# Reordering the linear pieces between a mixer's attentions, pacing the modulation by product work, and moving the first weight casts of a section

## The chip, the cores and the metric

The kernel runs on one core of a Trainium2 chip. The metric is the device time of one execution in microseconds (us). A run "before" means the kernel without the change; its median of three runs is 1349.51 us.

## The reference, cut to what matters

A trunk of two layers on one sequence of 256 tokens, 1024 wide. Each layer is a feed-forward half step, a token mixer, and a second feed-forward half step:

```python
def swiglu(h, w_gate, w_up, w_down):
    return (jax.nn.silu(h @ w_gate) * (h @ w_up)) @ w_down          # 1024 -> 2816 -> 1024
...
    proj = hn @ w_in                                                # 1024 -> 3488 + 3 * 1024 gates
    y_a = from_heads(moba_attention(...))                           # 256 tokens: causal softmax attention
    y_b = from_heads(stick_breaking_attention(qb_, kb_, vb_))
    qc = to_heads(rms_norm(c_q, q_norm) @ w_uq, MLA_HEADS)          # "up" products of the third attention
    kv = to_heads(rms_norm(c_kv, kv_norm) @ w_ukv, MLA_HEADS)
    y_c = from_heads(causal_softmax_attention(...))
    g = jax.nn.sigmoid(gates.reshape(bsz, s_len, N_BRANCH, D_MODEL) + b_gate)
    ys = jnp.stack([y_a, y_b, y_c], axis=2)
    merged = jnp.einsum('bsnk,nkd,bsnd->bsd', ys, w_branch, g)      # three branch products, each times its gate
    return merged @ w_out
...
    for l in range(DEPTH):
        mod = (c_act @ ada_w[l] + ada_b[l])                         # shift, scale, gate of each of the 3 sub-layers
        h = modulate(x, norm_pre[l, 0], mod[:, 0, 0], mod[:, 0, 1])
        x = residual_add(x, swiglu(h, ...), norm_post[l, 0], mod[:, 0, 2], 0.5)
        ...
```

Each of the 2 x 9 modulation vectors is a 1024 x 1024 matrix times one vector, some 75 MB of weights in all.

## The kernel before, in words

Everything lies transposed, 128 channels by 256 tokens to a tile. **Weights** come in pieces of 128 x 1024 f32 (512 KB) through one helper, `wsplit` (L144): SP issues the DMA into `raw` (L153, 5 buffers), ACT casts it to `whi` (L162, 6 buffers), DVE takes the difference `wlo` (L163, 6 buffers). **Products** are three matmuls each (L168 whi by hi, L169 whi by lo, L170 wlo by hi), called "lin"; a piece of 128 output channels from 1024 inputs is 24 matmuls of 256 columns. PSUM has 3 banks for lin, 4 for attention ("att"), one for sums ("sum").

**Modulation.** Behind the first two vectors, which the opening computes from its own loads (`oada`), 128 tiles `ada` of 512 KB are loaded by DMAs that POOL issues (L130, 2 buffers); each is reduced by one DVE instruction, the "dot" (L118). `ada_until(l, s, part)` emits loads and dots up to a share `part` of the 24 tiles that belong to a sub-layer. In the feed-forward it is called once per piece. In the mixer it is called by `progress()`, every second piece, with the count of pieces setting the share. A dot is held behind an "anchor", the last marked DVE instruction. The dots stand in DVE's queue in the place that this gives them, so a dot whose load has not landed holds up all of DVE.

**Mixer.** Three attentions run one after the other through `attend(fn, q, k, v, box, fill)`: stick-breaking (1), softmax (2, the MoBA branch), and softmax of the latent branch (3). Each has four pairs of heads in a pipeline of six steps; in each step a share of the list `fill` of independent linear pieces is emitted between the attention's own instructions. The kinds of pieces: `gate_pieces` (8 of 24 matmuls, evacuated by ACT, L482; behind the eighth one sigmoid over 128 x 2048, L484, between two table loads, L484 and L86), `branch_pieces` (8 of 12 matmuls, evacuated by DVE as a product with the gate, L498, and for branch 0 an addition, L733), `up_pieces` (12 short ones, evacuated by ACT: rot L689, yT L684, km L704, vm L711), `chunk_pieces` and `token_pieces`. After the third attention come branch 2 and the product with `w_out`, four groups of two output tiles, evacuated by `out_tile` (squares L213 and L308, yT L309, both ACT, and DVE for the last).

**Section changes.** `enter` normalises and modulates for the next section. Its list `hold` keeps instructions behind which the casts of the weights (both L162 and L163) must stand.

Instructions have the order that a scheduler gives them by the order in which the program emits them, with `issue_after` and `high_priority` as exceptions; on each engine they then run strictly in that order.

Of the kernel before, what the change touches and what calls it, by code (L numbers as in the profile page):

```python
# [12 lines left out]
F32R = mybir.dt.float32r  # L13
BF = mybir.dt.bfloat16
AF = mybir.ActivationFunctionType
# [4 lines left out]
S = 256  # L20
# [8 lines left out]
def trunk(ctx, tc, x, c, vecs, ada_w, w_gate, w_up, w_down, w_in, w_uq, w_ukv, w_branch, w_out, rope, out):  # L29
# [94 lines left out]
    def ada_until(l, s, part):  # L124

        n = min(24 * (3 * l + s) + int(24 * part), len(ada_todo))
        while ada_pos[0] < n:
            al, i, k = ada_todo[ada_pos[0]]
            raw = adap.tile([128, D], F32, name="ada")
            nc.gpsimd.dma_start(raw, ada_w[al, i * D + k * 128:i * D + k * 128 + 128, :])  # L130
            with tc.issue_after(anchor[-1].ins):
                ada_dot(raw, al, i, k)
            if k == KC - 1:
                nc.vector.tensor_add(modc[:, al, i, :], modc[:, al, i, :], adab[:, al, i * KC:i * KC + KC])
            ada_pos[0] += 1

    hold = []

    def block(src, at, kc, ncols):
# [163 lines left out]
    def out_tile(n, p, g):  # L303
        if n < KC - 1:
            if n < KC - 2:
                sum_sq(sqp, p, n == 0)
            else:
                nc.scalar.activation(sqm, p, AF.Square)  # L308
            nc.scalar.activation(yT[:, n, :], p, AF.Copy, scale=g[:, n:n + 1])  # L309
        else:  # L310
            nc.scalar.activation(sql, p, AF.Square)
            nc.vector.tensor_scalar(yT[:, n, :], p, g[:, n:n + 1], None, op0=OP.mult)
# [4 lines left out]
    def ffn(l, f, s, opening=None, ahead=None):  # L317
        with ExitStack() as es:
# [66 lines left out]
            for g in range(D // 256):  # L385
# [7 lines left out]
                for j in range(2):  # L393
                    out_tile(2 * g + j, pp[j], gc)
                ada_until(l, s, 1)


    def mixer(l, s):
        with ExitStack() as es:
# [184 lines left out]

            def attend(fn, q, k, v, box, fill):

                hi = mp.tile([128, 4, S], F32R, name="ybhi", bufs=2)
                lo = mp.tile([128, 4, S], F32R, name="yblo", bufs=2)
                box["act"] = lambda i, k: (hi, lo)[i][:, k, :]
                gens, wts = {}, {}  # L590
                NS = 6
                done, spent, total = 0, 0.0, sum(w for w, _ in fill)
                for t in range(NS):
                    n = t - 2
                    if n >= 0:
                        y = ps(S, kind="sum")
                        weighted(y, wts.pop(n), v, 2 * n)
                        nc.scalar.copy(hi[:, n, :], y)
                        nc.vector.tensor_sub(lo[:, n, :], y, hi[:, n, :].bitcast(F32))
# [5 lines left out]
                    while done < len(fill) and (spent < total * (t + 1) / NS or t == NS - 1):  # L605
                        spent += fill[done][0]
                        fill[done][1]()
                        done += 1
                        progress()

            steps = [0]

            def progress():
                steps[0] += 1
                if steps[0] % 2 == 0:
                    ada_until(l, s, min(1.0, max(0, steps[0] - 14) / 54))


            wb = [win(1536 + 256 * i, 256) for i in range(3)]
# [112 lines left out]
            def add_a(m):  # L732
                nc.vector.tensor_add(gb["g"][:, m, :], gb["g"][:, m, :], ga["g"][:, m, :])  # L733


            attend(softmax_pair, of64(qka, 0), of64(qka, 4), va, ya,
                   up_pieces() + gate_pieces(1, "ga", gb) + branch_pieces(1, yb, gb))


            attend(softmax_pair, lambda h: qm[:96, h, :], lambda h: km[:96, h, :], vm, yc,  # L740
                   gate_pieces(0, "gb", ga) + branch_pieces(0, ya, ga, add_a) + gate_pieces(2, "gb", gc))
            table_after(SQRT, last_exp[0], gc["sig"])

            def add_c(m):
# [4 lines left out]

            for _, piece in branch_pieces(2, yc, gc, add_c):  # L750
                piece()
            ada_until(l, s, 1)
            gcol = post_col(l, s, 1.0)
            for g in range(4):
                if g == 2:
# [7 lines left out]
                        lin(pp[j], w, k0, cols[j], hact, k0, nk, k0 == 0, k0 + nk == KC)  # L763
                for j in range(2):
                    out_tile(2 * g + j, pp[j], gcol)
                ada_until(l, s, 1)
        return ahead


# [189 lines left out]
```

## Time and profile before

| | |
|---|---|
| runs before, us | 1349.01, 1349.51, 1356.35 (median 1349.51) |
| the profiled execution, us | 1353.12 |
| its span, us | 1351.4 |
| mean granted TensorE clock | 0.984 of full speed |
| busy: PE / DVE / ACT / POOL | 96% / 73% / 56% / 5% |
| DMA | 295.75 MB, mean 219 GB/s |

All positions below are us from the start of that span. The profile names engines PE (TensorE), DVE (VectorE), ACT (ScalarE), POOL (GpSimd) and SP (SyncE). "out<-in" are the program's tiles. Behind an instruction the brackets give the idle time of its engine just ahead of it and the instruction or DMA that ended it. A busy PE need not be at full pace: the granted clock and the number of matmuls in a window tell that.

### The profile page before, as it was taken

To read this page: it belongs to the slowest core of one execution; us is meant where nothing else is said; L and a number is where in the kernel's file an instruction comes from. 1 tells how busy PE (TensorE), PEld (TensorE's weight loads), DVE (VectorE), ACT (ScalarE), POOL (GpSimd) and SP (SyncE) were. 2 spreads that over 40 slices of the span, in tenths; PEclk is the share of its full clock that TensorE was granted. 3 is DMA by queue.
4 is the path that set the end of the run, shared out by engine and by line. 5 is a ranking of instruction groups with operands and counts; after the bars stand their busy time and mean duration, and the time that the engine had idled before them with its cause. 6 is when DMAs were issued, how large, how long until landed. Compare 5 with 4: busy or idle time off the path is not lost.

```text
span 1351.4 us, 26656 instructions
## 1 busy us (share of the span) xinstructions
PE 1303.2 (96%) x10752; PEld 1269.9 (94%) x10752; DVE 986.4 (73%) x1706; ACT 755.7 (56%) x1287; POOL 69.5 (5%) x139
## 2 busy tenths in 40 slices
PE   6999989999899999999999999999998999999997
PEld 5999989998799999999999999999987999999997
DVE  7988766757768879876589775676686777885552
ACT  4554554766656656454565554467575756644551
POOL 0011000000101000110001110000010010000000
PEclk9999998999999999999999999999998999999998
DMA  9988872534866647887829887535366585285560
GB/s 362 343 296 305 281 263 91 188 104 163 287 200 221 229 140 248 306 289 248 274 61 319 292 286 251 195 121 169 118 227 206 194 291 202 80 316 187 173 198 32
DMA packets 82925, 295.75 MB, mean 219 GB/s; under 512 B 9201, under 2 KB 9585, under 8 KB 82802
## 3 DMA queue, kind: packets, MB, share of 16 engines
q1 hardware_dynamic: 64370, 226.94, 49.0%
q0 software_dynamic: 18432, 67.12, 15.1%
q8 instruction: 84, 1.38, 0.4%
q14 instruction: 39, 0.32, 0.1%
HBM read 292.97 MB, written 1.05 MB: 218 GB/s over the span
## 4 chain that ended last, share of the span: by engine, by line
issue 49%; PE 42%; DVE 3%; POOL 3%; DMA 2%; ACT 1%; SPq 0%; POOLq 0%; DVEq 0%; ACTq 0%
PE lin L168 11%; PE lin L170 11%; PE lin L169 11%; POOL ada L130 3%; PE att L823 1%; PE lin L273 1%; DMA ada<-in_ada_w_dram 1%; PE att L273 1%; PE lin L823 1%; PE sum L509 1%; DMA oada<-in_ada_w_dram 1%; PE att L519 1%; PE att L544 0%; DVE ada L118 0%; ACT whi L162 0%
## 5 line engine op out<-in xcount | busy, mean ns | idle before, releaser
L163 DVE TENSOR_TENSOR wlo<-raw,whi 128x1024 fp32r<-128x1024 f32 (+3 forms) x382 | 452.5, 1197 | 148.1 <-ACT whi L162 143.7
L162 ACT CAST whi<-raw 128x1024 fp32r<-128x1024 f32 (+3 forms) x382 | 391.3, 1032 | 227.0 <-PE lin L169 158.3
L170 PE MATMUL lin<-h,wlo 128*128 128x256 f32 x1808 | 510.4, 283 | 0.8 <-DVE wlo L163 0.8
L168 PE MATMUL lin<-h,whi 128*128 128x256 f32 x1808 | 510.9, 284 | 0.1
L169 PE MATMUL lin<-h,whi 128*128 128x256 f32 x1808 | 507.6, 282 | 0.2
L170 PEld LDWEIGHTS lin<-h,wlo 128*128 128x128 f32 x1808 | 341.4, 189 | 1.4 <-DVE wlo L163 1.4
L169 PEld LDWEIGHTS lin<-h,whi 128*128 128x128 f32 x1808 | 341.8, 189 | 1.0 <-DVE h L238 1.0
L168 PEld LDWEIGHTS lin<-h,whi 128*128 128x128 f32 x1808 | 340.4, 189 | 1.8 <-ACT h L237 1.0
L118 DVE SCALAR_TENSOR_TENSOR ada<-ada,cb 128x1024 f32<-128x1024 f32 x128 | 154.6, 1220 | 37.3 <-DMA ada<-in_ada_w_dram 37.0
L168 PE MATMUL lin<-mid,whi 128*128 128x256 f32 x592 | 163.6, 276 | 3.4 <-ACT yT L309 3.4
L170 PE MATMUL lin<-mid,wlo 128*128 128x256 f32 x592 | 163.5, 276 | 0.0
L169 PE MATMUL lin<-mid,whi 128*128 128x256 f32 x592 | 163.5, 276 | 0.0
L130 POOL DMA_DIRECT2D ada<-in_ada_w_dram x128 | 67.8, 530 | 1135.8 <-DVE ada L118 1103.3
L168 PEld LDWEIGHTS lin<-mid,whi 128*128 128x128 f32 x592 | 111.1, 188 | 3.6 <-ACT yT L309 3.6
L170 PEld LDWEIGHTS lin<-mid,wlo 128*128 128x128 f32 x592 | 111.2, 188 | 0.0
L169 PEld LDWEIGHTS lin<-mid,whi 128*128 128x128 f32 x592 | 111.2, 188 | 0.0
L346 ACT CAST mid<-m 128x256 fp32r<-128x256 f32 x88 | 34.7, 405 | 77.9 <-DVE m L342 77.5
L168 PE MATMUL lin<-ybhi,whi 128*128 128x256 f32 x192 | 56.2, 293 | 13.0 <-DVE ga L498 10.9
L169 PE MATMUL lin<-yblo,whi 128*128 128x256 f32 x192 | 54.6, 285 | 0.0
L170 PE MATMUL lin<-ybhi,wlo 128*128 128x256 f32 x192 | 54.5, 284 | 0.0
L168 PEld LDWEIGHTS lin<-ybhi,whi 128*128 128x128 f32 x192 | 37.5, 195 | 15.0 <-DVE ga L498 11.3
L273 PE MATMUL lin<-h,whi 128*128 128x258 f32 x240 | 46.7, 302 | 4.9 <-DVE h L262 4.9
(259 smaller groups left out, 1952.8 us busy)
## 6 DMA issues: line engine op xcount, KB each, us to landing
ada<-in_ada_w_dram POOLq DMA_DIRECT2D x128, 512.0 KB, 5.1
raw<-in_mix_w_in_dram SPq DMA_DIRECT2D x100, 512.0 KB, 5.1
raw<-in_ffn_w_gate_dram SPq DMA_DIRECT2D x88, 512.0 KB, 5.6
raw<-in_ffn_w_up_dram SPq DMA_DIRECT2D x88, 512.0 KB, 5.6
raw<-in_ffn_w_down_dram SPq DMA_DIRECT2D x80, 512.0 KB, 5.1
raw<-in_mix_w_branch_dram SPq DMA_DIRECT2D x24, 512.0 KB, 4.9
oada<-in_ada_w_dram SPq DMA_DIRECT2D x16, 512.0 KB, 7.4
raw<-in_mix_w_out_dram SPq DMA_DIRECT2D x16, 512.0 KB, 5.1
```

The source lines that it names most:

```text
L118: return nc.vector.scalar_tensor_tensor(raw, raw, 1.0, cb, op0=OP.mult, op1=OP.mult, accum_out=modc[:, l, i, k:k + 1])
L130: nc.gpsimd.dma_start(raw, ada_w[al, i * D + k * 128:i * D + k * 128 + 128, :])
L162: nc.scalar.copy(hi, raw)
L163: nc.vector.tensor_sub(lo, raw, hi.bitcast(F32))
L168: nc.tensor.matmul(o, whi, ahi, start=start, stop=False)
L169: nc.tensor.matmul(o, whi, alo, start=False, stop=False)
L170: nc.tensor.matmul(o, wlo, ahi, start=False, stop=stop)
L273: done.append(nc.tensor.matmul(p, w(i, k, cols), (hi, lo)[j], start=(k == 0 and i == j == 0), stop=(k == KC - 1 and j == 1)))
L346: nc.scalar.copy(mid[0][n], m)
L509: nc.tensor.matmul(y[64 * j:64 * j + 64, 128 * t:S], v[:, t, (h + j) * 64:(h + j) * 64 + 64], wT[j][:, 0:S] if t == 0 else wT[j][:, S:S + ...
L519: nc.tensor.matmul(scs[j][:, 128:384], q[j][:, 128:256], k[j][:, 0:256], start=False, stop=False, skip_group_check=True)
L823: nc.tensor.matmul(banks[j][:, a * 256:(a + 1) * 256], parts[k][a][i == 1][:, j * 128:(j + 1) * 128], hact(i == 2, k), start=(k == 0 and a ...
```

## The change

It has five parts. (1) The fill lists: attention 2 has gate 1, the up pieces and gate 0 instead of the up pieces, gate 1 and branch 1; attention 3 has branch 1, branch 0 and gate 2 instead of gate 0, branch 0 and gate 2. (2) `attend` allocates its result tiles `ybhi`/`yblo` in step 2 and not at its start, since three such pairs would be alive with two buffers. (3) `progress` gets a piece's weight (2.6 for 24 matmuls) and asks for `0.85 * (work - 16) / 105` of the 24 dots after every piece; the last dots are asked for behind the first and second group of `w_out` instead of ahead of `w_out`. (4) The first ada tile is written by a small POOL copy that reads the last modulation column of the opening, so its load, and all behind it on POOL, waits for the opening's last dot. (5) `out_tile` notes the evacuation of tile 5 as `late`, and at the end of a feed-forward and of a mixer `hold` is set to it, so the casts of the next section's first weights stand behind that evacuation.

```diff
@@ ada_until @@
             raw = adap.tile([128, D], F32, name="ada")
+            if ada_pos[0] == 0:
+                nc.gpsimd.tensor_copy(raw[:, 0:1], modc[:, 0, 0, KC - 1:KC])
             nc.gpsimd.dma_start(raw, ada_w[al, i * D + k * 128:i * D + k * 128 + 128, :])
...
+    late = []
     hold = []
@@ out_tile @@
-            nc.scalar.activation(yT[:, n, :], p, AF.Copy, scale=g[:, n:n + 1])
+            done = nc.scalar.activation(yT[:, n, :], p, AF.Copy, scale=g[:, n:n + 1])
+            if n == KC - 3:
+                late[:] = [done]
@@ ffn, at its end @@
                 ada_until(l, s, 1)
+            hold[:] = late
@@ attend @@
-                hi = mp.tile([128, 4, S], F32R, name="ybhi", bufs=2)
-                lo = mp.tile([128, 4, S], F32R, name="yblo", bufs=2)
-                box["act"] = lambda i, k: (hi, lo)[i][:, k, :]
...
                     n = t - 2
+                    if n == 0:
+                        hi = mp.tile([128, 4, S], F32R, name="ybhi", bufs=2)
+                        lo = mp.tile([128, 4, S], F32R, name="yblo", bufs=2)
+                        box["act"] = lambda i, k: (hi, lo)[i][:, k, :]
...
                         fill[done][1]()
+                        progress(fill[done][0])
                         done += 1
-                        progress()
-
-            steps = [0]
-
-            def progress():
-                steps[0] += 1
-                if steps[0] % 2 == 0:
-                    ada_until(l, s, min(1.0, max(0, steps[0] - 14) / 54))
+
+            work = [0.0]
+
+            def progress(w):
+
+                work[0] += w
+                ada_until(l, s, 0.85 * min(1.0, max(0.0, work[0] - 16) / 105))
@@ mixer @@
             attend(softmax_pair, of64(qka, 0), of64(qka, 4), va, ya,
-                   up_pieces() + gate_pieces(1, "ga", gb) + branch_pieces(1, yb, gb))
+                   gate_pieces(1, "ga", gb) + up_pieces() + gate_pieces(0, "gb", ga))
...
             attend(softmax_pair, lambda h: qm[:96, h, :], lambda h: km[:96, h, :], vm, yc,
-                   gate_pieces(0, "gb", ga) + branch_pieces(0, ya, ga, add_a) + gate_pieces(2, "gb", gc))
+                   branch_pieces(1, yb, gb) + branch_pieces(0, ya, ga, add_a) + gate_pieces(2, "gb", gc))
...
             for _, piece in branch_pieces(2, yc, gc, add_c):
                 piece()
-            ada_until(l, s, 1)
             gcol = post_col(l, s, 1.0)
...
-                ada_until(l, s, 1)
+                ada_until(l, s, 1 if g else 0.93)
+            hold[:] = late
```

**DVE, layer 0, up to the first branch-1 evacuations.** `gcol` is the mixer's post-norm column, `yblo` the low part of an attention result, `ga<-lin,ga` a branch-1 evacuation. Before:

```order
L297 SCALAR_TENSOR_TENSOR gcol<-modc,vecs 128x8
L118 SCALAR_TENSOR_TENSOR ada,modc<-ada,cb 128x1024
L163 TENSOR_TENSOR wlo<-raw,whi 128x1024
L118 SCALAR_TENSOR_TENSOR ada,modc<-ada,cb 128x1024
L599 TENSOR_TENSOR yblo<-sum,ybhi 128x256
L163 TENSOR_TENSOR wlo<-raw,whi 128x1024
L118 SCALAR_TENSOR_TENSOR ada,modc<-ada,cb 128x1024
L498 TENSOR_TENSOR ga<-lin,ga 128x256 x4
```

The same place now; line numbers are a few higher (L166 is `wlo`, L504 the branch evacuation, L537, L541 and L543 the softmax):

```order
L300 SCALAR_TENSOR_TENSOR gcol<-modc,vecs 128x8
L606 TENSOR_TENSOR yblo<-sum,ybhi 128x256
L166 TENSOR_TENSOR wlo<-raw,whi 128x1024 x4
L537 TENSOR_REDUCE nm<-att 128x1 x2
L504 TENSOR_TENSOR ga<-lin,ga 128x256 x3
L537 TENSOR_REDUCE nm<-att 128x1 x2
L504 TENSOR_TENSOR ga<-lin,ga 128x256
L166 TENSOR_TENSOR wlo<-raw,whi 128x1024
L541 RECIPROCAL r<-sm 128x2 x2
L504 TENSOR_TENSOR ga<-lin,ga 128x256
```

The dot that stood right ahead of the evacuations is elsewhere; softmax instructions of attention 3 now stand among them.

**ACT, layer 0, gate 1's last evacuation and the first two pairs of up pieces** (`rot`, `yT`), now:

```order
L488 ACTIVATE ga<-lin,vecs 128x256
L165 CAST whi<-raw 128x1024
L490 ACT_TABLE_LOAD
L490 ACTIVATE ga<-ga 128x2048
L86 ACT_TABLE_LOAD
L696 ACTIVATE rot<-lin 128x256 x2
L691 ACTIVATE yT<-lin 64x256 x2
L605 CAST ybhi<-sum 128x256
L691 ACTIVATE yT<-lin 64x256 x2
L552 COPY wT<-att 128x384
L691 ACTIVATE yT<-lin 64x256 x4
L552 COPY wT<-att 128x384
```

Before, what followed gate 1's sigmoid on ACT was the attention's own work and casts, with branch 1 on DVE:

```order
L482 ACTIVATE ga<-lin,vecs 128x256
L598 CAST ybhi<-sum 128x256
L484 ACT_TABLE_LOAD
L484 ACTIVATE ga<-ga 128x2048
L86 ACT_TABLE_LOAD
L546 COPY wT<-att 128x384 x2
L162 CAST whi<-raw 128x1024 x2
L598 CAST ybhi<-sum 128x256
```

The block of table load, sigmoid and table load has moved from ahead of casts and copies to ahead of the up evacuations, which free PE's lin banks.

**ACT, the end of the first feed-forward** (with the numbers of the tiles, since rows read alike; `lin_2238` and `lin_2239` hold output tiles 4 and 5). Before:

```order
L162 CAST wd16_0_2536<-raw_2542 128x512
L162 CAST whi_2597<-raw_2595 128x1024
L162 CAST whi_2603<-raw_2601 128x1024
L213 ACTIVATE sq_2408<-lin_2238 128x256
L309 ACTIVATE yT_139<-lin_2238,gcol_1865 128x256
L162 CAST whi_2609<-raw_2607 128x1024
```

Now:

```order
L165 CAST wd16_0_2537<-raw_2543 128x512
L216 ACTIVATE sq_2409<-lin_2239 128x256
L312 ACTIVATE yT_139<-lin_2239,gcol_1866 128x256
L216 ACTIVATE sq_2413<-lin_2240 128x256
L312 ACTIVATE yT_139<-lin_2240,gcol_1866 128x256
L165 CAST whi_2598<-raw_2596 128x1024
```

The casts of the mixer's first weights have moved from ahead of the evacuation of tile 4 to behind that of tile 5.

## Rows read from the trace of the kernel before

**Rows 1.** The page, part 1: busy time, share of the span and instructions of each engine.

```profile
PE 1303.2 (96%) x10752; PEld 1269.9 (94%) x10752; DVE 986.4 (73%) x1706; ACT 755.7 (56%) x1287; POOL 69.5 (5%) x139
```

**Rows 2.** PE's waits over the span: line waited at, instruction waited for, us in total, times, longest.

```profile
PE lin L168 <- DVE ga L498: 10.9, 2, 6.3
...
PE lin L168 <- ACT yT L309: 3.4, 1, 3.4
...
PE lin L168 <- DVE gb L498: 2.0, 2, 1.0
PE lin L168 <- ACT yT L684: 1.5, 4, 0.6
```

**Rows 3.** Windows at the end of attention 2 of layer 0 (363 to 378 us) and layer 1 (1023 to 1035 us). Columns: from and to, length, busy us (and instructions) of PE, weight loads, DVE, ACT, POOL; granted clock; DMA share; GB/s.

```profile
363.30:368.10 4.80, 0.15 (x3) 0.03 (x1) 2.19 (x5) 1.27 (x3) 0.12 (x1) 0.80 0.98 373
368.10:373.10 5.00, 5.00 (x23) 4.07 (x24) 2.64 (x5) 2.46 (x3) 0.40 (x1) 0.51 0.62 202
373.10:378.10 5.00, 5.00 (x46) 5.00 (x45) 2.24 (x5) 0.46 (x1) 0.00 (x0) 1.00 0.67 212
1023.40:1029.80 6.40, 0.18 (x2) 0.00 (x0) 2.58 (x5) 1.33 (x3) 0.40 (x2) 0.89 0.88 319
1029.80:1035.20 5.40, 5.36 (x24) 4.43 (x25) 3.04 (x5) 2.46 (x3) 0.47 (x1) 0.50 0.31 102
```

**Rows 4.** The timeline of DVE in the same two places: start, us, instruction, and in brackets the idle time ahead of it and what ended it.

```profile
366.45 1.23 DVE L118 SCALAR_TENSOR_TENSOR ada<-ada,cb 128x1024 f32<-128x1024 f32 x1 [2.60 <-DMA ada<-in_ada_w_dram]
...
367.60 1.08 DVE L498 TENSOR_TENSOR ga<-lin,ga 128x256 f32<-128x256 f32 x3
...
1028.22 1.23 DVE L118 SCALAR_TENSOR_TENSOR ada<-ada,cb 128x1024 f32<-128x1024 f32 x1 [3.82 <-DMA ada<-in_ada_w_dram]
```

**Rows 5.** The timeline of POOL: the first two ada loads, and the load that the dot at 366.45 us reads.

```profile
2.06 0.67 POOL L130 DMA_DIRECT2D ada<-in_ada_w_dram  x1
...
2.98 0.55 POOL L130 DMA_DIRECT2D ada<-in_ada_w_dram  x1
...
360.39 0.53 POOL L130 DMA_DIRECT2D ada<-in_ada_w_dram  x1 [3.04 <-DVE ada L118]
```

**Rows 6.** The timelines of ACT and PE at the end of the first feed-forward.

```profile
193.47 1.05 ACT L162 CAST whi<-raw 128x1024 fp32r<-128x1024 f32 x1 [2.26 <-DMA raw<-in_mix_w_in_dram]
195.59 1.04 ACT L162 CAST whi<-raw 128x1024 fp32r<-128x1024 f32 x1 [1.07 <-DMA raw<-in_mix_w_in_dram]
196.54 0.38 ACT L213 ACTIVATE sq<-lin 128x256 f32<-128x256 f32 x1
...
197.33 0.39 PE L168 MATMUL lin<-mid,whi 128*128 128x256 f32 x1 [3.43 <-ACT yT L309]
```

**Rows 7.** One window of the opening (columns as in rows 3).

```profile
5.00:10.00 5.00, 1.16 (x2) 0.00 (x0) 2.26 (x5) 1.02 (x3) 0.00 (x0) 1.00 1.00 380
```

**Rows 8.** The timeline of DVE at its first dot of the opening.

```profile
12.72 1.22 DVE L118 SCALAR_TENSOR_TENSOR oada<-oada,cb 128x1024 f32<-128x1024 f32 x1 [1.06 <-DMA oada<-in_ada_w_dram]
```

**Rows 9.** Two windows in the mixer of layer 0 (columns as in rows 3): the up pieces, and eight branch-0 pieces in attention 3.

```profile
317.40:328.80 11.40, 10.60 (x77) 8.45 (x75) 10.47 (x23) 10.01 (x31) 0.53 (x1) 1.00 0.30 93
411.00:423.00 12.00, 11.97 (x103) 11.09 (x103) 11.85 (x30) 9.25 (x18) 0.53 (x1) 1.00 0.79 260
```

**Rows 10.** ACT's instructions by line and shape, 300 to 460 us: count, busy us, mean ns of one, idle ahead.

```profile
L162 ACT CAST whi<-raw 128x1024 fp32r<-128x1024 f32 x42 | 43.8, 1054 | 24.0 <-PE lin L169 21.8 <-PE lin L170 2.1
...
L482 ACT ACTIVATE ga<-lin,vecs 128x256 f32<-128x256 f32 x8 | 3.9, 487 | 2.0 <-PE lin L170 2.0
...
L684 ACT ACTIVATE yT<-lin 64x256 f32<-64x256 f32 x8 | 3.0, 378 | 0.1
L704 ACT COPY km<-lin 64x256 f32<-64x256 f32 x8 | 2.9, 368 | 0.1
...
L711 ACT COPY vm<-lin 128x512 f32<-128x512 f32 x2 | 1.2, 596 | 0.0
...
L689 ACT ACTIVATE rot<-lin 128x256 f32<-128x256 f32 x2 | 0.8, 383 | 0.6 <-PE lin L170 0.6
```

**Rows 11.** The timeline of ACT at gate 1's sigmoid, layer 0.

```profile
359.19 1.28 ACT L484 ACT_TABLE_LOAD   x1
360.49 1.92 ACT L484 ACTIVATE ga<-ga 128x2048 f32<-128x2048 f32 x1
362.42 1.28 ACT L86 ACT_TABLE_LOAD   x1
363.72 0.86 ACT L546 COPY wT<-att 128x384 f32<-128x384 f32 x2
```

**Rows 12.** DVE's instructions by line and shape, 395 to 460 us.

```profile
L163 DVE TENSOR_TENSOR wlo<-raw,whi 128x1024 fp32r<-128x1024 f32 x17 | 20.5, 1220 | 3.9 <-ACT whi L162 3.9
L118 DVE SCALAR_TENSOR_TENSOR ada<-ada,cb 128x1024 f32<-128x1024 f32 x10 | 12.1, 1221 | 3.5 <-DMA ada<-in_ada_w_dram 3.5
L498 DVE TENSOR_TENSOR gb<-lin,gb 128x256 f32<-128x256 f32 x15 | 5.9, 415 | 2.4 <-ACT gb L484 2.4
L733 DVE TENSOR_TENSOR ga<-ga,gb 128x256 f32<-128x256 f32 x8 | 3.2, 415 | 0.0
```

**Rows 13.** Windows at two section changes (columns as in rows 3).

```profile
215.00:220.00 5.00, 5.00 (x28) 5.00 (x27) 5.00 (x15) 2.88 (x8) 0.00 (x0) 0.56 0.02 3
475.00:500.00 25.00, 23.45 (x193) 22.97 (x193) 18.63 (x43) 13.14 (x31) 0.00 (x0) 1.00 0.31 106
```

## The prediction

> **What bounds the kernel now.** I began with the busy line [rows 1]. PE is busy for 96% of the span, DVE for 73%, ACT for 56%, so a change that leaves the products alone can only win back stretches where PE stands or is slowed. PE's waits say where these are [rows 2]: the longest are two on a DVE evacuation (10.9 us together), and there is one of 3.4 us on an ACT evacuation. The windows [rows 3], the timelines of DVE, POOL and ACT [rows 4 to 6] and the orders of the two programs then show what stands ahead of these evacuations. The profiled execution took 1353.12 us (span 1351.4), 3.6 us over the median of the runs, 1349.51, which is inside their spread; the sum below is a difference made on that trace, and I take it off the median. About 0.5% (1342.8 to 1356.3) is what a measurement of this kernel can tell from no change.
>
> **Part 1, fill lists and pace of the modulation: what goes.** At the end of attention 2 the first branch-1 evacuations stand on DVE right behind a dot. That dot ran at 366.45 us, released by its load, which POOL had issued at 360.39 [rows 4, 5]: some 6 us from issue to use, at a DMA share of 0.98. PE ran 3 matmuls in the 4.80 us to 368.10. Five us of half clock (0.51) follow, with 23 matmuls where the next five have 46 [rows 3]. Cost: 4.8 less 3 x 0.11 = 4.5 idle, and 2.5 of slow clock, 7.0 together. In layer 1, 2 matmuls in 6.40 us are 6.2 idle; 24 in 5.40 us, where full pace gives some 50, are 2.8; together 9.0. Both layers: 16.0.
>
> In the changed order no dot stands just ahead of the evacuations: behind the last one come `gcol`, four differences and two softmax reductions. The old pace asked for 24 x 2 / 54 = 0.9 dots per two pieces, whatever their size, which among branch pieces of 12 matmuls is a dot per 24 matmuls, some 2.7 us. The new one asks for 0.85 x 24 / 105 dots per unit of work, one in 5.15 units, that is in two pieces of 24 matmuls, about 5.3 us of products and more with the attention's own. With two buffers a load then has some 11 us, against the 6 seen. So I take the whole **-16.0**. What is late next are the four differences of branch weights, which wait for casts and loads, as the same instructions do everywhere else without holding PE.
>
> **Part 1, what it adds: gate 1's sigmoid ahead of the up pieces.** Before, behind that block on ACT stood casts and copies, while branch 1 was freed by DVE. Now the twelve up pieces stand behind it, and these free PE's three lin banks only through ACT. Count from the end of gate 1's last product. ACT: evacuation 0.49, one cast 1.05 [rows 10], table load, sigmoid, table load 1.28 + 1.92 + 1.28 = 4.48 [rows 11]: 6.0. Then two rot (0.77), eight yT (3.02) and six of the eight km (2.21) [rows 10], 6.0 more, and the attention's share. That I read from the up stretch before: ACT was busy 10.01 us there [rows 9], of which some 7.9 are up evacuations (the 0.77, 3.02, 2.94 and 1.2 for vm [rows 10]), so 2.1 is left for exponentials and copies. The bank for the last product is free at 6.0 + 6.0 + 2.1 = 14.1, and PE is through at about 15.0. PE's work in that time: before, the stretch had 77 matmuls in 11.40 us; at the pace of 103 in 12 us [rows 9] that is 9.0 of work and 2.4 already lost. One group of weighted sums more makes 9.9. So 15.0 - 9.9 = 5.1 is lost, 2.7 more than before. Bounds for a layer: 0 (the attention's matmuls cover the block; a gain is excluded, as the evacuations that cost 2.4 all stay) and 5.5 (block and cast lie open). I take 2.7, **+5.4** for two layers.
>
> Beside this number stands a rule of the Trainium skill. The rows show the sigmoid starting 0.02 us behind the end of its table load, and the copy behind the second load likewise (362.42 + 1.28 = 363.70, next start 363.72) [rows 11]: a switch costs 1.28 and nothing else. The Trainium skill, "ScalarE: Activation LUTs", section "What ACT_TABLE_LOAD costs", says that a load of about 1283 ns is followed by a drain of about 1380 ns, 2.66 us for every switch. The trace agrees on the load and shows no drain; by the page the sum would have some 2.8 us more in each layer.
>
> **Part 1, what it adds: branch evacuations among the softmax of attention 3.** Sixteen branch pieces now lie in its first three steps, where before eight lay. A branch-1 evacuation takes DVE 0.415 us, a branch-0 one with its addition 0.83, a difference 1.22, a dot 1.22 [rows 12]. With eight of the dearer kind DVE was busy 11.85 of 12.00 us and PE still had 103 matmuls [rows 9], so DVE is just enough. The lighter eight come first and save 3.3 us against a second such stretch. What can hold PE is an evacuation queued behind a softmax instruction that waits for ACT. The nearest row is PE's wait on gate 0's or 2's branch evacuations, 1.0 us each, two in the span [rows 2]. Bounds for a layer: 0 and three such waits, 3.0. A gain is excluded, since PE did not wait there before. I take one, **+2.0** for both layers. Moving the allocation of `ybhi` and `yblo` into step 2 adds no instruction: 0.
>
> **Part 2, the last dots behind w_out's groups.** Four dots stand now among `w_out`'s evacuations, two behind the first group and two behind the second. Each group is 48 matmuls, 5.3 us, so two groups are left when the last is asked for, and nothing but the next section reads the result: 0. If that cover were gone, the price would be one load, 6 us.
>
> **Part 3, the opening.** Two ada loads of 512 KB were issued at 2.06 and 2.98 us [rows 5] and ran among the loads of x and of the first dots, with all DMA engines busy at 380 GB/s [rows 7]. Taken out they free 1.05 MB / 380 GB/s = 2.8 us. DVE waited 1.06 us for its first dot's load at 12.72 [rows 8], behind work that waited for x. The gain lies between 0 (nothing shortens but the queue's tail) and 2.8; I take **-2.0**, nearer the upper end, as both the loads of x and those of the dots lie behind the same megabyte. POOL's new copy waits for the opening's last dot, and behind it in POOL's queue is only the chain of ada loads. These then start with the first feed-forward's pieces, whose pace is unchanged.
>
> **Part 4, casts behind tile 5.** At the end of the first feed-forward two casts of mixer weights wait 2.26 and 1.07 us for their loads, and the evacuation of tile 4 (0.38 at 196.54) stands behind them. PE waits 3.43 us [rows 6]. With the casts behind tile 5 it goes: **-3.4**. Those casts start some 4 us later; six of 1.05 are done by about 204, while the last group of 132 matmuls runs to about 212, so PE's next need is covered by 8 us. At the two mixer ends three or four casts now stand between the evacuations of tiles 5 and 6. There the groups are short, 5.3 us, and up to one cast, 1.05, can be late: bounds 0 and 1.05 each, half taken as nothing tells which, **+1.0**.
>
> **Sum.** -16.0 - 2.0 - 3.4 + 5.4 + 2.0 + 1.0 = -13.0. On the profiled execution 1340.1; from the median 1349.5 - 13.0 = **1336.5 us**.
>
> **Rivals.**
> - *ACT and DVE give the gain back.* Both added terms at their upper ends, with 1.0 at each mixer end: (5.5 + 3.0 + 1.0) x 2 = 19.0 against 21.4 won, 1347.1. For it: ACT already limited PE in the up stretch, and DVE had no idle time to spare at 411 us. Against: PE has attention work and three banks to run ahead in.
> - *The late dot moves into attention 3.* Its dots stand between branch evacuations, as they did at the end of attention 2. One late dot in each layer costs what the old stall cost, 16.0: 1352.5, no change that can be told. Two in each layer, the **other side**, cost 32.0: 1368.5, slower. It decides from the point where a load takes more than the 11 us of two dots' pace. For it: the loads of branch 1, branch 0 and gate 2 follow each other there. Against: 6 us was seen at a DMA share of 0.98, and at 411 to 423 us, with a share of 0.79, PE did not wait.
> - *A table switch costs more than its row.* If ACT stood for another 1.28 us behind each load once evacuations are queued there, 2.6 a layer come on top: 1336.5 + 5.1 = 1341.6. That is the way of the page of the Trainium skill named above; both switches in the rows speak against it.
> - *The change doesn't do what it says*: the pace or the hold leaves the dots and casts where they were. The orders show them moved. 1349.5.
>
> **How the numbers follow.** Forecast 0.68; giving back 0.14; one late dot a layer 0.07; two 0.07; table switch 0.02; no effect 0.02. Faster by over 0.5%: 0.68 + 0.02 = 0.70. Within 0.5%: 0.14 + 0.07 + 0.02 = 0.23. Slower: 0.07. The range's low end has the three added terms at zero (1336.5 - 8.4 = 1328.1), the opening at 2.8 (1327.3), and one stretch of half clock less at a section change, where 28 matmuls ran in 5 us instead of 43 at full pace, while another change passed with the clock at 1.00 [rows 13]: some 1.8, to 1325. The high end takes in the giving back, 1347. Outside lie one and two late dots, 0.14, and a little of the forecast's tails.
>
> **What would show it.** Right: no PE wait on branch evacuations over 2 us at the end of attention 2 or in attention 3, granted clock 1.00 through both; no wait at tile 4 of the first feed-forward; the first dot of the opening near 10.7 us; some 5 us lost in the up pieces, waited for on rot, yT and km. Wrong: a dot in attention 3 with an idle time of several us ahead of it, released by its load; a half clock behind the up pieces, which would add to their 2.7; an opening whose first dot is still at 12.7.

## The result, and the profile after

| | before | after |
|---|---|---|
| median, us (runs) | 1352.93 (4) | 1336.57 (4) |
| lowest to highest | 1349.01 to 1358.08 | 1335.89 to 1339.09 |
| profiled execution, us | 1353.12 | 1337.06 |
| ratio | | 0.9877, 95% interval 0.9841 to 0.9913 |

The kernel is faster by 1.2% (0.9 to 1.6%). The time forecast was 1336.5. The two profiled executions differ by 16.1 us, where the sum had said 13.0; so the sum was 3.1 short, and the median of three that it was taken off, 1349.51, was 3.4 lower than that of all four (in later series before had medians of 1353.4 to 1355.1). Part of the closeness is luck: these two cancel. One of the six runs of the kernel with the up pieces first, below, took 2100.7 us at a granted clock of 0.56, and its ratio leaves that run out (the median of the other five is 1328.71).

What PE waits for now, in PE's waits over the span (answers to [rows 2]):

```profile
PE lin L171 <- ACT rot L696: 3.4, 2, 1.7
...
PE lin L171 <- DVE m L347: 2.1, 3, 1.1
PE lin L171 <- DVE gb L504: 2.0, 2, 1.0
```

The two waits on branch-1 evacuations, 10.9 us together, and the 3.4 us on tile 4 are gone. New are 1.7 us in each layer on `rot`, the first up piece, and waits on `m`, which is an evacuation of the feed-forward. The first was forecast, the second was not.

**The place where the stall was.** The timeline of DVE in the changed kernel, in the gate-0 pieces of attention 2 of both layers (answers to [rows 4]), and windows of PE around them (columns as in [rows 3]):

```profile
373.18 1.23 DVE L118 SCALAR_TENSOR_TENSOR ada<-ada,cb 128x1024 f32<-128x1024 f32 x1 [3.39 <-DMA ada<-in_ada_w_dram]
...
1027.14 1.22 DVE L118 SCALAR_TENSOR_TENSOR ada<-ada,cb 128x1024 f32<-128x1024 f32 x1 [3.03 <-DMA ada<-in_ada_w_dram]
```

```profile
369.00:374.00 5.00, 5.00 (x45) 4.61 (x43) 1.61 (x2) 2.95 (x4) 0.00 (x0) 1.00 1.04 402
1022.00:1027.00 5.00, 5.00 (x44) 5.00 (x43) 2.12 (x2) 2.82 (x4) 0.53 (x1) 1.00 0.99 365
```

Dots are late as ever, by 3.4 and 3.0 us, with all DMA engines busy. But PE runs 44 or 45 matmuls in these 5 us at full clock: behind the late dot stand no evacuations that PE needs, since gate pieces are freed by ACT. POOL issued the loads of these two dots here:

```profile
365.48 0.53 POOL L132 DMA_DIRECT2D ada<-in_ada_w_dram  x1 [3.66 <-DVE ada L118]
...
1019.86 0.53 POOL L132 DMA_DIRECT2D ada<-in_ada_w_dram  x1 [3.82 <-DVE ada L118]
```

From issue to use that is 7.7 and 7.3 us, and DVE had come to the dots 4.3 us after the issue, in both layers.

**The up pieces.** The timeline of ACT from the cast behind gate 1's last evacuation on (layer 0, answers to [rows 11]), and windows of that stretch in layer 0 and 1:

```profile
343.11 1.05 ACT L165 CAST whi<-raw 128x1024 fp32r<-128x1024 f32 x1
344.19 1.28 ACT L490 ACT_TABLE_LOAD   x1
345.48 1.91 ACT L490 ACTIVATE ga<-ga 128x2048 f32<-128x2048 f32 x1
347.41 1.28 ACT L86 ACT_TABLE_LOAD   x1
348.70 0.66 ACT L696 ACTIVATE rot<-lin 128x256 f32<-128x256 f32 x2
...
354.40 2.29 ACT L711 COPY km<-lin 64x256 f32<-64x256 f32 x6
```

```profile
344.50:361.00 16.50, 14.65 (x96) 11.55 (x95) 11.78 (x27) 15.91 (x38) 0.89 (x2) 0.90 0.30 96
350.00:354.00 4.00, 4.00 (x21) 3.67 (x20) 3.89 (x8) 3.61 (x12) 0.00 (x0) 0.57 0.17 69
999.00:1015.50 16.50, 13.94 (x99) 10.44 (x98) 12.05 (x27) 16.17 (x38) 0.87 (x2) 1.00 0.29 96
```

ACT is busy 15.9 and 16.2 of 16.5 us and PE gets through 96 and 99 matmuls, where the stretch before had 77 in 11.4 [rows 9]. The cast ends at 344.16 and six km evacuations at 356.69: 12.5 us, where the prediction had 14.1 - 1.5 = 12.6. The instruction behind each table load starts 0.01 us after its end, much as in [rows 11], so the drain that the Trainium skill names ("ScalarE: Activation LUTs", "What ACT_TABLE_LOAD costs") does not show here either. Behind the wait for rot the clock falls to 0.57 in layer 0; in the second profile of the same kernel it falls in both layers.

**The opening and the end of the first feed-forward.** The timeline of DVE at the first dot of the opening (answers to [rows 8]), and that of ACT at tiles 4 and 5 (answers to [rows 6]):

```profile
9.90 1.22 DVE L118 SCALAR_TENSOR_TENSOR oada<-oada,cb 128x1024 f32<-128x1024 f32 x1
```

```profile
191.23 0.38 ACT L216 ACTIVATE sq<-lin 128x256 f32<-128x256 f32 x1
191.50 0.47 ACT L312 ACTIVATE yT<-lin,gcol 128x256 f32<-128x256 f32 x1
192.12 0.38 ACT L216 ACTIVATE sq<-lin 128x256 f32<-128x256 f32 x1 [0.15 <-PE lin L173]
192.41 0.47 ACT L312 ACTIVATE yT<-lin,gcol 128x256 f32<-128x256 f32 x1
194.08 1.05 ACT L165 CAST whi<-raw 128x1024 fp32r<-128x1024 f32 x1 [1.20 <-DMA raw<-in_mix_w_in_dram]
```

The first dot starts at 9.90 in place of 12.72, and without a wait. The evacuations run first, and the cast then waits for its load by itself.

**What was not forecast.** The timeline of DVE in the first feed-forward of the changed kernel:

```profile
107.26 1.22 DVE L118 SCALAR_TENSOR_TENSOR ada<-ada,cb 128x1024 f32<-128x1024 f32 x1 [4.06 <-DMA ada<-in_ada_w_dram]
...
120.62 1.23 DVE L118 SCALAR_TENSOR_TENSOR ada<-ada,cb 128x1024 f32<-128x1024 f32 x1 [3.09 <-DMA ada<-in_ada_w_dram]
...
124.04 0.42 DVE L347 TENSOR_TENSOR m<-lin,sg 128x256 f32<-128x256 f32 x1
```

Here late dots do stand ahead of what PE needs (`m`), and PE lost over 3 us by them: its matmul behind the `m` of 124.04 starts at 124.5. The program there is the same before and after.

**Where the 16 us came from.** The table gives, for several kernels, the time PE lost in stretches that hold the same work: for each pair of successive matmuls the time between their starts, less what it is at full pace for the columns of the first (0.117 us for 256), summed. It counts waits and slow clock alike. It is worked out from all of each trace's matmul records.

| PE's loss, us | opening | first ffn behind it, up to the third group of its down product | rest of its down product | attention 2 to first branches, layer 0 | the same, layer 1 | attention 3 and w_out, both layers | the three changes at the mixers | total |
|---|---|---|---|---|---|---|---|---|
| before | 16.3 | 1.2 | 3.6 | 12.6 | 15.4 | 10.7 | 14.8 | 107.7 |
| after | 13.8 | 4.7 | -0.2 | 7.9 | 7.3 | 11.2 | 15.6 | 91.9 |
| after, second profile | 13.2 | 4.0 | 0.3 | 8.2 | 8.0 | 10.9 | 16.0 | 93.6 |
| fill lists alone | 16.4 | 4.7 | 2.7 | 8.4 | 8.1 | 15.7 | 14.8 | 104.1 |
| pace alone | 16.2 | 6.9 | 1.4 | 6.8 | 6.6 | 10.7 | 18.8 | 99.2 |
| opening alone | 13.0 | 1.2 | 1.9 | 14.1 | 15.8 | 10.9 | 10.4 | 100.4 |
| hold alone | 16.3 | 5.3 | -0.2 | 15.2 | 14.8 | 10.9 | 13.9 | 108.2 |
| after, up pieces first | 13.4 | 3.6 | -0.2 | 5.4 | 4.9 | 11.4 | 11.6 | 83.2 |
| the same, second profile | 13.1 | 4.7 | -0.2 | 5.4 | 4.9 | 11.0 | 12.4 | 84.3 |

"The three changes" are from the first ffn to the first mixer, and from each mixer to the ffn behind it; the remaining stretches, not shown, agree within 2 us. Half clock at the changes comes and goes between executions. The second column is called the gate and up part below, and the third the down product; the border lies near the 1400th matmul. The 1.2 us of before in the second column hold no wait for an evacuation: matmuls of 256 columns follow each other every 0.120 us in the gate and up pieces and every 0.113 us in the down product, both at a granted clock of 1.00, and the sum takes 0.117 for both. So differences between rows are what to read.

### The profile page after: what moved, and what is told of

It is laid out like the page before. It is cut to its first block, busy times and chain, and to the rows that moved or that the text cites. A ratio compares the mean times of both kernels' runs of the same rounds, so it can differ in the third digit from the quotient of the medians.

```text
span 1335.3 us, 26637 instructions
## 1 busy us (share of the span) xinstructions
PE 1300.3 (97%) x10752; PEld 1267.3 (95%) x10752; DVE 985.5 (74%) x1706; ACT 754.9 (57%) x1287; POOL 70.6 (5%) x140
## 3 DMA queue, kind: packets, MB, share of 16 engines
q0 software_dynamic: 18432, 67.12, 15.2%
## 4 chain that ended last, share of the span: by engine, by line
PE 60%; DVE 3%; ACT 3%; DMA 0%; issue 0%; SPq 0%
PE lin L173 17%; PE lin L171 17%; PE lin L172 17%; PE lin L276 3%; PE att L276 2%; PE sum L515 1%; PE sum L190 1%; ACT whi L165 1%; DVE h L241 1%; DVE pn L238 1%; DMA raw<-in_mix_w_out_dram 0%; DVE wlo L166 0%; PE att L550 0%; PE sum L204 0%; PE att L525 0%
## 5 line engine op out<-in xcount | busy, mean ns | idle before, releaser
L166 DVE TENSOR_TENSOR wlo<-raw,whi 128x1024 fp32r<-128x1024 f32 (+3 forms) x382 | 451.4, 1196 | 139.6 <-ACT whi L165 137.9
L352 DVE TENSOR_TENSOR mid<-m,mid 128x256 fp32r<-128x256 f32 x88 | 36.2, 421 | 20.6 <-ACT mid L351 20.6
```

Of the source, the lines that this page charges most:

```text
L166: nc.vector.tensor_sub(lo, raw, hi.bitcast(F32))
L352: anchor[:] = [nc.vector.tensor_sub(mid[1][n], m, mid[0][n].bitcast(F32))]
```

## The experiments

**Fill lists alone.** Before, with the new lists and late allocation of the result tiles, the old pace, opening and casts.

```diff
-                   up_pieces() + gate_pieces(1, "ga", gb) + branch_pieces(1, yb, gb))
+                   gate_pieces(1, "ga", gb) + up_pieces() + gate_pieces(0, "gb", ga))
...
-                   gate_pieces(0, "gb", ga) + branch_pieces(0, ya, ga, add_a) + gate_pieces(2, "gb", gc))
+                   branch_pieces(1, yb, gb) + branch_pieces(0, ya, ga, add_a) + gate_pieces(2, "gb", gc))
```

> Before, with the fill lists of the change (and the result tiles allocated in step 2) but the old pace of the modulation, the old opening and no hold. Theory 'pace' (the stall at the end of attention 2 goes because dots come less densely): dots still stand among branch-1 evacuations, now in attention 3, so PE waits there for DVE for some 4 to 6 us in a layer with a half clock behind; the time stays within 4 us of before. Theory 'place' (it goes because a late dot now stands among gate-0 pieces, which ACT frees, so PE does not care): no PE wait on a branch evacuation over 1.5 us, both stalls of 7.0 and 9.0 us gone, the up pieces lose 2.8 and 1 us more, 11 to 13 us less than before.

Measured: 1348.27 us (before 1355.11), ratio 0.9936 (0.9914 to 0.9958). PE's waits:

```profile
PE lin L168 <- ACT rot L690: 3.4, 2, 1.7
PE lin L168 <- DVE m L342: 2.7, 3, 1.5
...
PE lin L168 <- DVE gb L498: 2.5, 2, 1.5
PE sum L509 <- DVE yblo L600: 2.4, 2, 1.3
...
PE lin L169 <- DVE yblo L600: 1.0, 1, 1.0
```

The stall is gone with the old pace too, and no wait on a branch evacuation over 1.5 us came in attention 3: "place" holds. DVE's timeline has dots late by 2.9 and 3.8 us among the gate-0 pieces at the end of attention 2 (the first branch piece starts at 390.4 and 1046.4 us), and PE has no wait there; the third row is from attention 3 of layer 1:

```profile
381.09 1.22 DVE L118 SCALAR_TENSOR_TENSOR ada<-ada,cb 128x1024 f32<-128x1024 f32 x1 [2.94 <-DMA ada<-in_ada_w_dram]
...
1038.02 1.23 DVE L118 SCALAR_TENSOR_TENSOR ada<-ada,cb 128x1024 f32<-128x1024 f32 x1 [3.76 <-DMA ada<-in_ada_w_dram]
...
1098.95 1.22 DVE L118 SCALAR_TENSOR_TENSOR ada<-ada,cb 128x1024 f32<-128x1024 f32 x1 [2.98 <-DMA ada<-in_ada_w_dram]
```

But the gain is 7 (1355.11 less 1348.27), not 11 to 13: attention 3 and `w_out` lost 5.0 us more (15.7 against 10.7), most of it in layer 1, where dots are late by up to 3.0 us and PE then waits for `yblo` (1.0 us at 1105 us) and `gb` (1.5). So the new place needs the new pace; in the full change attention 3 costs next to nothing.

**Pace alone.** Before, with dots paced by product work and the last four behind groups of `w_out`.

```diff
+                        progress(fill[done][0])
...
+                work[0] += w
+                ada_until(l, s, 0.85 * min(1.0, max(0.0, work[0] - 16) / 105))
...
-                ada_until(l, s, 1)
+                ada_until(l, s, 1 if g else 0.93)
```

> Before, with the new pace of the modulation alone (share by product work, last four dots behind groups of w_out). Theory 'pace': the two stalls at the end of attention 2 go, 14 to 16 us less than before, no loss in the up pieces. Theory 'place': a dot of this stretch is still late by 2 to 4 us with the branch evacuations behind it, half of the stalls or more stays, 0 to 8 us less than before.

Measured: 1342.72 us, ratio 0.9895 (0.9866 to 0.9924). DVE's timeline at the old place of the stall, and PE's waits:

```profile
364.86 1.23 DVE L118 SCALAR_TENSOR_TENSOR ada<-ada,cb 128x1024 f32<-128x1024 f32 x1 [1.40 <-DMA ada<-in_ada_w_dram]
...
1019.13 1.23 DVE L118 SCALAR_TENSOR_TENSOR ada<-ada,cb 128x1024 f32<-128x1024 f32 x1 [1.47 <-DMA ada<-in_ada_w_dram]
```

```profile
PE lin L168 <- DVE m L342: 4.0, 6, 1.5
...
PE lin L168 <- DVE ga L498: 1.9, 2, 1.0
```

Lateness fell from 2.6 and 3.8 [rows 4] to 1.4 and 1.5, PE's wait to 1.0 in each layer, and the two stretches lost 5.8 and 8.8 us less. So "pace" holds as well: either part alone takes most of the same stall, and their gains don't add. The medians differ by 12.4 us, where 14 to 16 were expected: the two stretches gave 14.6, with 2 us of waits left, and in this profile the first feed-forward (5.7 in the gate and up part) and the section changes (4.0) lost more than before.

**Opening alone.**

```diff
             raw = adap.tile([128, D], F32, name="ada")
+            if ada_pos[0] == 0:
+                nc.gpsimd.tensor_copy(raw[:, 0:1], modc[:, 0, 0, KC - 1:KC])
```

> Before, with the first ada load put behind the opening alone. In the change the opening won 2.5 us and the first feed-forward lost 3.2 us by two waits on DVE behind late dots (at 107 and 121 us). Theory 'debt' (DMA bounds the first 150 us, so the megabyte taken out of the opening has to be loaded later, and late dots pay for it): the opening is 2.5 us shorter, the same waits appear before 160 us, and by 190 us the gain is gone, net -0.5 to +1. Theory 'separate' (those waits come from elsewhere): 2 to 3 us less than before at 190 us and at the end.

Measured: 1353.45 us, ratio 0.9981 (0.9951 to 1.0012), not told from no change by its runs, which spread from 1345.6 to 1362.3. By its trace the opening lost 13.0 us and not 16.3, and the gate and up part lost 1.2, as before: no debt in this execution. All eight profiles with this part lost 13.0 to 14.3 in the opening, all four without it 16.2 to 16.4; so the 2 to 3.3 us are the part's. The waits of the first feed-forward are missing here and stand in the three other kernels of this series, which lack this part (4.7, 6.9 and 5.3 us): "debt" falls, they are from elsewhere. That the 2 to 3 us are left at the end, the times don't show.

**Hold alone.**

```diff
+            if n == KC - 3:
+                late[:] = [done]
...
+            hold[:] = late
```

> Before, with the hold of the first casts behind the evacuation of tile 5 alone. The theory: the wait of 3.4 us at the end of the first feed-forward goes, the mixer ends cost 0 to 1 us each, in all 2 to 4 us less than before. Rival (the six casts behind tile 5 come too late for the mixer's first products): a new wait of PE on whi or wlo of 1 to 3 us at 210 us, no gain.

Measured: 1354.24 us, ratio 0.9987 (0.9968 to 1.0007), again within the runs' spread. In the trace the down product of the first feed-forward lost 3.8 us less than before (-0.2 against 3.6), no wait on whi or wlo came at the change, and the gate and up part lost 5.3 where before had 1.2, in a program that is the same there. That hid the gain in this profile, and the times show none. The gain depends on how late the loads are: without the hold, three other kernels lost 2.7, 1.4 and 1.9.

**The changed kernel again.**

> The changed kernel once more, beside the three that follow. Theory: the waits of PE on DVE in the first feed-forward (100 to 160 us) differ from execution to execution, since a kernel with the identical program there lost 0 to 5.6 us in five profiles. Then its time lies in 1333 to 1340 us, and its profile may show these waits or not. Rival: they belong to the changed kernel, then they come again with 2 to 4 us, at the same pieces.

Measured: 1338.29 us (before 1354.44), ratio 0.9884 (0.9867 to 0.9901). Of the waits of the first feed-forward the last came again, at the same pieces (1.1 us, where the down product starts); the earlier ones did not. The gate and up part lost 4.0 us, 2.8 over before: 1.4 by this wait, and 1.4 because the matmuls of the down product came more slowly (45 in 5 us from 150 us on, where the first profile has 47, both at a granted clock of 1.00). Over the ten profiles that have this program there (with or without the opening's part), the loss is 1.2, 1.2, 3.6, 4.0, 4.7, 4.7, 4.7, 5.3, 6.3 and 6.9 us. Two of them, before and "opening alone", have no wait on `m` there, the others 1.1 to 4.0 us in all. The kernels with one part of the change each show that it varies by execution and is not the change's, and the profile before was one of the lightest. Why an execution is light or heavy stays open.

**Up pieces first**, as before the change, with gate 0 behind gate 1.

```diff
-                   gate_pieces(1, "ga", gb) + up_pieces() + gate_pieces(0, "gb", ga))
+                   up_pieces() + gate_pieces(1, "ga", gb) + gate_pieces(0, "gb", ga))
```

> The changed kernel with the up pieces ahead of gate 1 in attention 2, as before, and gate 0 behind gate 1. Theory of the prediction (gate 1's sigmoid on ACT holds the up evacuations): no wait of PE on rot, the up stretch loses 2.4 us in a layer as before and not 4 to 5, no half clock behind it; 4 to 5 us less than the changed kernel, and the stall on branch evacuations stays gone. Rival (ACT bounds this stretch whatever the order, and the sigmoid ahead of gate-0 pieces holds these in turn): the loss moves behind gate 1, as a wait on gb's evacuations of 2 to 3 us a layer; within 2 us of the changed kernel.

Measured: 1328.84 us beside the changed kernel's 1338.29, ratio to before 0.9809 (0.9791 to 0.9827). PE's waits have no rot any more:

```profile
PE lin L171 <- DVE gb L504: 2.0, 2, 1.0
...
PE lin L171 <- DVE m L347: 1.7, 2, 1.3
PE lin L171 <- ACT yT L691: 1.5, 4, 0.6
```

The wait on yT is that of [rows 2]. The clock stays at 1.00 through these stretches, and they lost 5.4 and 4.9 us, where the changed kernel's two profiles have 7.9 and 7.3, and 8.2 and 8.0. That is 4.9 to 5.9 of the 9.4 us; the rival is out. A further 4 lies at the three section changes (15.6 and 16.0 against 11.6 and 12.4), where less half clock was seen; its cause is open.

**No fill lists**, all else of the change.

```diff
-                   gate_pieces(1, "ga", gb) + up_pieces() + gate_pieces(0, "gb", ga))
+                   up_pieces() + gate_pieces(1, "ga", gb) + branch_pieces(1, yb, gb))
...
-                   branch_pieces(1, yb, gb) + branch_pieces(0, ya, ga, add_a) + gate_pieces(2, "gb", gc))
+                   gate_pieces(0, "gb", ga) + branch_pieces(0, ya, ga, add_a) + gate_pieces(2, "gb", gc))
```

> The changed kernel without its fill lists: old order of the pieces, with the new pace, opening and hold. Theory: the pace alone removes the stall at the end of attention 2 (it did alone: 5.8 and 8.8 us), and the up pieces are not behind the sigmoid; so 3 to 5 us less than the changed kernel, some 1332 us. Rival (the pace is marginal: in this order a dot that is late still stands ahead of branch evacuations): PE waits of 1 to 4 us on branch-1 evacuations in one layer or both, equal to the changed kernel or slower, with a wider spread of its runs.

Measured: 1336.22 us, ratio 0.9866 (0.9847 to 0.9886), within 2.1 us of the changed kernel. PE's waits:

```profile
PE lin L171 <- DVE m L347: 2.7, 4, 1.3
...
PE lin L171 <- DVE ga L504: 2.0, 2, 1.3
PE lin L171 <- ACT yT L690: 1.5, 4, 0.6
```

The rival is nearer: the waits on branch-1 evacuations are there, 1 us a layer, and the runs spread wider (6.0 us against 2.8). The two stretches lost 6.6 and 6.9 us, together 1.7 and 2.7 less than in the changed kernel's two profiles, but 3.2 more than with the up pieces first. Pace is marginal in the old order; the best is the new place with the up pieces first.

**Dots of the first feed-forward spread over its down product.**

```diff
-                ada_until(l, s, 0.9 * i / len(todo))
+                ada_until(l, s, (0.9 if opening is None else 0.5) * i / len(todo))
...
-                ada_until(l, s, 1)
+                ada_until(l, s, 1 if opening is None else min(1, 0.7 + 0.2 * g))
```

> The changed kernel with the dots of the first feed-forward spread over its down product too: up to 0.5 of the 24 dots in the gate and up pieces (0.9 before), the rest behind the groups of the down product. Theory (late dots ahead of the products' evacuations cause these waits): no wait of PE on m over 0.5 us before 160 us, 1 to 4 us less than the changed kernel and a narrower spread. Rival (loads of weights, not dots, bound that stretch, the dots only show it): waits on wlo or whi come in their place, no gain.

Measured: 1340.98 us, ratio 0.9905 (0.9888 to 0.9921), its median 2.7 slower than the changed kernel's. The waits on m are gone (1.1 us of loss in that stretch), as forecast, but not the gain: a dot late in the down product holds the differences, these hold the casts on ACT, and behind the casts stands the evacuation that the section's end needs. PE's waits, and the timelines of DVE and ACT there:

```profile
PE sum L190 <- ACT sqm L311: 5.4, 1, 5.4
```

```profile
203.74 1.23 DVE L118 SCALAR_TENSOR_TENSOR ada<-ada,cb 128x1024 f32<-128x1024 f32 x1 [5.04 <-DMA ada<-in_ada_w_dram]
```

```profile
210.71 1.04 ACT L165 CAST whi<-raw 128x1024 fp32r<-128x1024 f32 x1 [5.65 <-DVE wlo L166]
211.66 0.38 ACT L311 ACTIVATE sqm<-lin 128x256 f32<-128x256 f32 x1
```

**Fewer dots moved, and up pieces first.** 0.75 in place of 0.5; the rest behind the first two groups.

```diff
+                ada_until(l, s, (0.9 if opening is None else 0.75) * i / len(todo))
...
+                ada_until(l, s, 1 if opening is None else min(1, 0.92 + 0.09 * g))
```

> The changed kernel with the up pieces ahead of gate 1, and in the first feed-forward up to 0.75 of the dots in the gate and up pieces, four more behind the first group of the down product and two behind the second, so that none is left for its end. Theory (late dots cause the waits on m, and the harm in the version with 0.5 came from the dots late in the down product): waits on m in 100 to 160 us of 0 to 1 us against 1.6 to 3.6, none at the end of the section; 1 to 2 us less than the same kernel with 0.9. Rival (the stretch is bound by loads): no difference, or the wait comes up in the down product, 0 to 3 us more.

Measured: 1329.54 us, ratio 0.9830 (0.9802 to 0.9857). The trace shows no wait on m and none at the section's end: 1.2 us lost in the gate and up part and -0.2 in the down product. Both profiles with fewer dots there have no wait on m; of the ten with 0.9 two have none. With the timeline above, where `m` stands behind a late dot, that makes late dots the cause of these waits. Yet the time is that of the kernel beside it:

> The changed kernel with the up pieces ahead of gate 1 once more, on the chip of the version with fewer dots: 1325 to 1331 us if the gain over the changed kernel is of the order of the pieces. If part of it was chance in the first feed-forward and at the section changes, up to 1334 us.

Measured: 1329.42 us, ratio 0.9841 (0.9811 to 0.9870). Against the two profiles with 0.9 the version with fewer dots stands 2.3 and 3.1 us better at the end of the first feed-forward, and gives that back in half clock at the two mixer ends, 1.9 to 2.3 and 0.8 to 1.2. Whether that follows from the edit or from the execution is open; no gain is shown.

## Why the prediction was right, term by term

- **The stall at the end of attention 2, -16.0.** Right in size, 1.7 short: with the up pieces out of the way the two stretches lost 7.2 and 10.5 us less. Of the two reasons given, one held: no dot stands just ahead of the evacuations any more, and what keeps PE going is the late dots' place among pieces that ACT frees. The other failed: "with two buffers a load then has some 11 us, against the 6 seen". Where the dots are late, by 3.4 and 3.0 us, DVE came to them 4.3 us after the issue of their loads, and these took 7.7 and 7.3 us to be used. The 11 us took the dots to be evenly spaced, one in 5.3 us; in the trace five in a row start at 358.63, 359.77, 363.95, 366.28 and 373.18 us. Pace alone took 14.6; place alone took the stall and gave 5.0 back in attention 3.
- **Up pieces behind gate 1's sigmoid, +5.4.** Measured 4.9 and 5.9 in the traces, by moving them back. The count of ACT's instructions, 12.6 us from the cast's end to the sixth km, came within 0.1 of the trace. What it left out is the half clock, listed among the signs of being wrong: it came, and added little. In the first profile layer 0 had it and layer 1 did not, and they lost 2.5 and 2.4 us more than with the up pieces first; in the second both had it, for 2.8 and 3.1.
- **Attention 3, +2.0, and the mixer ends, +1.0.** Over-sized: 0.2 to 0.5 in both layers together for the first, and no wait on a tile's evacuation for the second (the three section changes lost 0.8 and 1.2 more than before, with half clock in them). Both were halves or single steps between bounds.
- **The opening, -2.0.** Measured 2.5 and 3.1 in the two profiles of the changed kernel. "Nearer the upper end" was right; the whole 2.8 would have been better.
- **Casts behind tile 5, -3.4.** Measured 3.8 and 3.3 against the profile before.
- **A term that was missing, +2.8 to +3.5:** the first feed-forward, by late dots in the first profile of the changed kernel, and in its second half by them and half by slower matmuls. It belongs to the execution and not to the change. The profile taken before had no such wait.

From the table, before to after: opening -2.5, gate and up of the first feed-forward +3.5, its down product -3.8, the two stretches of attention 2 -4.7 and -8.1 (the stall's -17.7 and the up pieces' +4.9), attention 3 and `w_out` +0.5, section changes +0.8: -14.3. The remaining stretches, whose program is the same, make it -15.8; the spans differ by 16.1. Against the forecast's sum the stall gave 1.7 more, the opening and the casts 0.9 more, attention 3 and the section changes cost 1.7 less, the up pieces 0.5 less, and the missing term took 3.5 back. The last 1.8 lie in stretches whose program is the same (1.5) and outside the matmuls (0.3); what they are is not shown.

## What to carry to other kernels

An instruction that may wait for a load should stand, in its engine's queue, ahead of work that nobody needs soon: move it, or move what stands behind it to another engine; spacing the loads helps too, but these two remedies take the same microseconds once. When pieces are reordered, look at what frees the banks: a block on the freeing engine (here 4.5 us of table loads and sigmoid) in front of twelve short pieces cost 2.4 to 3.1 us a layer, and in front of long pieces PE had no wait. One profile is one draw: stretches that depend on when loads land differed by up to 5.7 us between executions of the same program, so a term should be taken from several.

## What the runs showed of the hardware that was not expected

- The stretch of the first feed-forward with the same program lost between 1.2 and 6.9 us; PE's waits behind late dots in it sum to 0 to 4.0 us, and a dot was late by up to 4.1 us. Runs of one kernel spread by up to 17 us (1345.6 to 1362.3, the last at a granted clock of 0.94), most of all in the kernels with the old stall.
- At a granted clock of 1.00, matmuls of 256 columns came every 0.120 us in the gate and up pieces of the first feed-forward and every 0.113 us in its down product, and in two of twelve profiles every 0.118 us there (267 matmuls in 150 to 180 us before, 257 in the changed kernel's second profile). The cause is open.
- The granted clock fell to half behind a stretch where PE lost about a third of its time in pieces of up to 1.7 us (0.57 in 350 to 354 us, and 0.61 in the second profile of the same kernel). One continuous wait of 3.4 us before, at 193 to 197 us, was followed by a clock of 1.00, and so was the same wait for rot in layer 1 of the first profile, with 21 matmuls in 1000 to 1004 us; the stall of 4.8 us of [rows 3] was followed by 0.51.
